# State space stage and branch projection of a streaming encoder layer, rewritten as one program in fixed order

## The chip, the cores and the metric

The kernel runs on one core of one Trainium2 chip. The metric is the device time of one execution in microseconds (us). Several runs of a kernel are taken and the median is given; one execution more is recorded by the hardware profiler, with the start of every instruction.

The engines are written as in the profile: PE (TensorE, matrix products; PEld its weight loads), DVE (VectorE), ACT (ScalarE), POOL (GpSimd), SP (SyncE, which here only issues DMAs). Each engine works through its own queue in order and waits for others by semaphores.

## What is computed

One layer of a hybrid trunk, for 256 frames of a new stream and 8 x 16 frames of running streams: 384 tokens in all, model width 2048, fp32.

```
u = rmsnorm(x)
proj = u @ w_in                      # pool | z | xBC | dt | gates
A = pooling branch(pool part)
xBC = silu(causal_conv(xBC) + b)     # width 4, per channel
x, B, C = split(xBC)                 # 64 heads of 64, 8 groups, state 128
y, h = ssd_scan(x, dt, A, B, C, h0)  # h: one 64x128 state a head
y = y + d_skip * x
y = rmsnorm over each group of 512 (y * silu(z)) * gain
m = sigmoid(gA) * (A @ w_pool_proj) + sigmoid(gB) * (y @ w_ssd_proj)
x += rmsnorm(m @ w_out)
x += rmsnorm(relu(rmsnorm(x) @ w_up)**2 @ w_down)
```

The scan of a group and chunk: `cb = C Bt`; for each head `Y = (cb * decay) @ (x dt) + exp(cum) * (C @ h)`; `h = h * exp(last) + Bt @ (x dt w_end)`. Outputs are the two token blocks and the new pooling, convolution and scan states.

## The kernel before

**Layout.** Activations lie transposed: a tile is 128 channels x 384 tokens, 256 of the new stream and 8 x 16 of the running ones. Every large product is done in two fp32r parts for accuracy: weights and activations are each split into a high part (ACT copy to fp32r) and a low part (DVE difference), and three products high x high, high x low, low x high are accumulated (`mm3`, L79 to L82). A *unit* is 512 KB of weights, 128x1024: SP fetches it (`wfetch`, L61), ACT and DVE split it (`wsplit`, L66 to L73), TensorE does 8 x 3 products of 384 columns with it (`half`, L84). Three buffers serve each of raw, high and low weights.

**Stages.** Pooling branch and gate A; then the state space stage (`phd`, from L371); then the branch projection (`phe`, from L612: 16 tiles of 4 units each, merged with the gates); then `w_out`; then the MLP. The state space stage goes through 8 groups. In each: conv tiles B and C, four conv tiles x (`conv`, L390: scale by rstd, four taps, Silu), four z tiles, one gate B tile in the first six groups (`NG = 6`), two units each. The last ten gate tiles come at the end.

**Short products.** When a group's tiles are there, plain fp32 products follow: the transposes of B (`trB`, L437), `cb` = B x C (L461), and for each of four pairs of heads j the transposes of x (`trx`, L480), `yi` = C x state (L514, in four strips of 32 columns), `Y` (L531, two strips of 64 columns; the scaled `yis` is added by a product with the identity, L539), and `pp`, the new prompt state (L560). An fp32 product appears in the trace as two records. After every second pair, `xhl` goes through DRAM (`x_scr`) into the strided tile `xst`, and eight fp32r products `su` (L587) update 1 MB of running states `hs`, which is stored and its buffer loaded anew. `b_scr` and `bst` do the same for B. The decays E are made per head by one ACT Exp, three DVE differences (L499), and two Exps for the pair; DVE multiplies them by the masked `cb` (L509).

**Norm of a group.** `finish` (L592) calls `rms_bc` (L113): three fp32 products of the sum of squares with two columns of ones (`st`, L116), Newton's steps for 1/sqrt on a 128x3 tile, three diagonal tiles `dg`, one fp32 product of ones with them (`bc`, L125) that spreads the result over the partitions; then four DVE products scale z into `a_scr` in DRAM.

**Order.** In all of this the order of instructions on each engine is not the program's: a scheduler places them by its own estimates of when operands are ready and of priority, so short products fall between units of dense ones wherever it finds them ready. Only the MLP runs in written order, under `tc.manual_schedule()`. PSUM's eight banks are four for long products (`mm`) and four for short ones (`ss`).

Of the kernel before, what the change touches and what calls it, by code (L numbers as in the profile page):

```python
# [27 lines left out]
NG = 6  # L28
# [6 lines left out]
def build(ctx, tc, io):  # L35
# [5 lines left out]
    psm = ctx.enter_context(tc.tile_pool(name="psm", bufs=4, space=PSUM))  # L41
    pss = ctx.enter_context(tc.tile_pool(name="pss", bufs=4, space=PSUM))
# [7 lines left out]
    def mmtile(name):  # L50
        return psm.tile([P, 512], F32, tag="mm", name=name)

    def sstile(name):
        return pss.tile([P, 512], F32, tag="ss", name=name)
# [20 lines left out]

    def wload(src, name):
        return wsplit(wfetch(src, name))
# [293 lines left out]
    with tc.tile_pool(name="phd", bufs=2, reuse_waits="tile") as pd, tc.tile_pool(  # L371
        name="phd1", bufs=1, reuse_waits="tile"
    ) as pd1:
        bst = []
        for i in range(2):
            b = pd1.tile([P, 4, 2, P], F32R, name=f"bst{i}")
            gp.memset(b.bitcast(F32), 0.0)
            bst.append(b)
        cst_ = pd1.tile([P, 48, 9, 3], F32, name="cstate")
        gp.dma_start(cst_, io["state_conv"])  # L380
        cbuf = []
        for i in range(3):
            b = pd1.tile([P, 24, 19], F32, name=f"cbuf{i}")
            gp.memset(b[:, 0, :3], 0.0)
            cbuf.append(b)
        seg = lambda a: a.rearrange("p (b t) -> p b t", b=24)
        ncv = [0]

        def conv(ui, c, tag, nb):
            ps = proj(in_units(ui), xg, f"x{c}")  # L390
            b = cbuf[ncv[0] % 3]
            ncv[0] += 1
            v.tensor_tensor(b[:, :, 3:], seg(ps), seg(rstd), ALU.mult)
            s.copy(b[:, 16:, :3], cst_[:, c, 1:])
            s.copy(b[:, 1:16, :3], b[:, 0:15, 16:])
            s.copy(cst_[:, c], b[:, 15:, 16:])
            a = pd.tile([P, T], F32, tag="cacc", name=f"cacc{c}")
            w = lambda j: vec[:, V_CW + c * 4 + j : V_CW + c * 4 + j + 1]
            v.tensor_scalar(seg(a), b[:, :, 0:16], w(0), None, ALU.mult)
            for j in range(1, 4):  # L400
                v.scalar_tensor_tensor(
                    out=seg(a), in0=b[:, :, j : j + 16], scalar=w(j), in1=seg(a), op0=ALU.mult, op1=ALU.add
                )
            o = pd.tile([P, T], F32, tag=tag, name=f"xs{c}", bufs=nb)
            s.activation(o, a, AF.Silu, bias=vec[:, V_CB + c : V_CB + c + 1])
            return o

        gates = list(range(16))

        def gate_b():  # L410
            n = gates.pop(0)
            ps = proj(in_units(33 + n), xg, f"gb{n}")
# [5 lines left out]
        for g in range(G):  # L418
            u0 = 49 + g * 10
            BT = conv(u0, 32 + g, "BT", 2)  # L420
            CT = conv(u0 + 1, 40 + g, "CT", 2)
            xs = []
            for j in range(4):
                xs.append(conv(u0 + 2 + j, g * 4 + j, "xs", 6))
                if g and j == 2:
                    finish(last[0])
            zs = []
            for j in range(4):
                ps = proj(in_units(u0 + 6 + j), xg, f"z{g}_{j}")
                z = pd.tile([P, T], F32, tag="zs", name=f"zs{g}_{j}", bufs=7)  # L430
                v.tensor_tensor(z, ps, rstd, ALU.mult)
                s.activation(z, z, AF.Silu)
                zs.append(z)

            tr = sstile(f"trB{g}")
            for b in range(3):
                te.transpose(tr[:, b * P : b * P + P], BT[:, b * P : b * P + P], ident)  # L437
            Bk = pd.tile([P, 2, P], F32, tag="Bk", name=f"Bk{g}")
            s.copy(Bk.rearrange("p b n -> p (b n)"), tr[:, :TP])
            Bhl = pd.tile([P, 2, P], F32R, tag="Bhl", name=f"Bhl{g}", bufs=1)  # L440
            s.activation(Bhl[:, 0, :], tr[:, TP:T], AF.Copy)
            v.tensor_tensor(Bhl[:, 1, :], tr[:, TP:T], Bhl[:, 0, :].bitcast(F32), ALU.subtract)
            bscr = b_scr[g]
            sy.dma_start(bscr, Bhl.bitcast(F32))
            bs = bst[g % 2]
            for p4 in range(4):
                for h2 in range(2):
                    sy.dma_start(
                        bs[p4 * 32 + h2 * 16 : p4 * 32 + h2 * 16 + 16, :, h2, :].bitcast(F32),
                        bscr.rearrange("(q h r) l n -> h l r q n", q=4, h=2)[h2, p4 // 2],  # L450
                    )
            Cm = pd.tile([P, 2, P], F32, tag="Cm", name=f"Cm{g}")
            v.tensor_tensor(
# [14 lines left out]
            for j in range(4):  # L468
# [10 lines left out]
                for b in range(3):  # L479
                    te.transpose(tr[:, b * P : b * P + P], xs[j][:, b * P : b * P + P], ident)  # L480
# [124 lines left out]
        while gates:  # L605
            gate_b()
# [612 lines left out]
```

## Time and profile before

| | |
|---|---|
| runs | 2835.02, 2835.99, 2837.01 us |
| median | 2835.99 us |
| profiled execution | 2835.97 us, of which span 2834.2 us |
| PE busy | 2811.6 us, 99% of the span |
| DVE busy | 1797.7 us, 63% |
| ACT busy | 1278.2 us, 45% |
| POOL busy | 251.2 us, 9% |
| mean DMA rate | 174 GB/s |

The span is the time from the first to the last instruction of the profiled execution; what lies around it belongs to the launch. A row of instructions reads: line, engine, operation, tile written <- tiles read (buffer numbers left out), shape, count | busy us, mean ns of one | idle time of the engine before them and what ended it. Matmul records overlap, since they are pipelined: their starts are measured, their ends are modelled. So the price of a product is the time from its start to the next one's start, not its length. A row of stages gives the stretch, its length, and each engine's busy time with the number of instructions in the order PE, PEld, DVE, ACT, POOL, then TensorE's granted clock, the DMA share and GB/s.

### The profile page before, as it was taken

The page shows a single profiled execution, that of the slowest core. Times are in us where ns is not written, and L with a number is a line of the kernel's source. Part 1 is how long each engine was busy: PE and PEld are TensorE (multiplying, and loading weights), DVE is VectorE, ACT ScalarE, POOL GpSimd, SP SyncE. Part 2 cuts the span into 40 slices and gives each one's busy share as a digit, 9 for nine tenths or more (in the row PEclk, how much of TensorE's full clock was granted, in tenths as well). Part 3 has the DMA queues.
Part 4 walks back from the last instruction along what each step waited for, and adds up shares of the span by engine and source line. Part 5 has one row for each costly group of instructions (what it writes and reads, how often), then busy time and mean ns, then how long its engine had stood idle before and what let it go on. Part 6 is the DMA issues. An engine that isn't in the chain of part 4 may idle for free.

```text
span 2834.2 us, 40535 instructions
## 1 busy us (share of the span) xinstructions
PE 2811.6 (99%) x15997; PEld 2655.8 (94%) x15997; DVE 1797.7 (63%) x2504; ACT 1278.2 (45%) x1866; POOL 251.2 (9%) x321
## 2 busy tenths in 40 slices
PE   9999999999999999999999999999999999999998
PEld 8999999999999999999999988899999999999996
DVE  7774335678677677686633333666767677676766
ACT  5443224345445455343522223545555555555553
POOL 0000000011011011011000000000111111111111
PEclk9999999999999999999999999999999999999999
DMA  6444445466465465565744454445666656666656
GB/s 212 134 133 142 138 138 196 142 208 208 148 219 193 158 224 178 169 234 185 244 149 149 154 182 130 149 167 172 186 184 158 163 160 167 167 180 188 182 131 233
DMA packets 160784, 492.90 MB, mean 174 GB/s; under 512 B 19809, under 2 KB 43553, under 8 KB 155729
## 3 DMA queue, kind: packets, MB, share of 16 engines
q1 hardware_dynamic: 133296, 410.14, 43.8%
q0 software_dynamic: 27296, 80.18, 11.8%
q8 instruction: 125, 2.05, 0.3%
q14 instruction: 67, 0.54, 0.1%
HBM read 412.34 MB, written 77.89 MB: 173 GB/s over the span
## 4 chain that ended last, share of the span: by engine, by line
PE 97%; DVE 1%; DMA 0%; ACT 0%; issue 0%; SPq 0%; DVEq 0%; ACTq 0%
PE pj_up L80 6%; PE pj_up L81 6%; PE pj_up L82 6%; PE pj_x L82 5%; PE pj_x L80 5%; PE pj_x L81 5%; PE wd L914 3%; PE pj_sp L80 3%; PE wd L916 3%; PE pj_z L82 3%; PE wd L915 3%; PE pj_z L80 3%; PE pj_sp L81 3%; PE pj_z L81 3%; PE pj_sp L82 3%; PE t L914 2%
## 5 line engine op out<-in xcount | busy, mean ns | idle before, releaser
L80 PE MATMUL pj_up<-x1h,wh_up 128*128 128x384 f32 x1024 | 345.6, 338 | 0.0
L81 PE MATMUL pj_up<-x1l,wh_up 128*128 128x384 f32 x1024 | 345.2, 337 | 0.0
L82 PE MATMUL pj_up<-x1h,wl_up 128*128 128x384 f32 x1024 | 344.6, 337 | 0.0
L80 PE MATMUL pj_x<-xgh,wh_x 128*128 128x384 f32 x768 | 261.4, 340 | 0.0
L82 PE MATMUL pj_x<-xgh,wl_x 128*128 128x384 f32 x768 | 258.3, 336 | 0.0
L81 PE MATMUL pj_x<-xgl,wh_x 128*128 128x384 f32 x768 | 256.9, 334 | 0.0
L73 DVE TENSOR_TENSOR wl_wd<-raw,wh_wd 128x1024 fp32r<-128x1024 f32 x168 | 202.2, 1222 | 68.9 <-ACT wh_wd L71 65.3
L71 ACT ACTIVATE wh_wd<-raw 128x1024 fp32r<-128x1024 f32 x168 | 175.1, 1054 | 97.0 <-PE pj_up L81 84.3
L80 PEld LDWEIGHTS pj_up<-x1h,wh_up 128*128 128x128 f32 x1024 | 192.8, 188 | 4.8 <-ACT x1h L732 0.4
L81 PEld LDWEIGHTS pj_up<-x1l,wh_up 128*128 128x128 f32 x1024 | 192.8, 188 | 4.5
L82 PEld LDWEIGHTS pj_up<-x1h,wl_up 128*128 128x128 f32 x1024 | 192.7, 188 | 0.1
L82 PE MATMUL pj_z<-xgh,wl_z 128*128 128x384 f32 x512 | 171.0, 334 | 0.0
L80 PE MATMUL pj_z<-xgh,wh_z 128*128 128x384 f32 x512 | 171.0, 334 | 0.0
L82 PE MATMUL pj_sp<-abh,wl_sp 128*128 128x384 f32 x512 | 171.0, 334 | 0.0
L81 PE MATMUL pj_z<-xgl,wh_z 128*128 128x384 f32 x512 | 171.0, 334 | 0.0
L80 PE MATMUL pj_sp<-abh,wh_sp 128*128 128x384 f32 x512 | 171.0, 334 | 0.0
L81 PE MATMUL pj_sp<-abl,wh_sp 128*128 128x384 f32 x512 | 171.0, 334 | 0.0
L73 DVE TENSOR_TENSOR wl_sp<-w_sp,wh_sp 128x1024 fp32r<-128x1024 f32 x64 | 78.2, 1224 | 118.3 <-ACT wh_sp L71 117.9
L882 POOL DMA_DIRECT2D acc_scr<-ev x108 | 92.9, 930 | 667.7 <-ACT ev L878 650.8
L80 PEld LDWEIGHTS pj_x<-xgh,wh_x 128*128 128x128 f32 x768 | 144.3, 188 | 2.5 <-issue 1.4
L82 PEld LDWEIGHTS pj_x<-xgh,wl_x 128*128 128x128 f32 x768 | 144.2, 188 | 2.6 <-issue 2.6
L81 PEld LDWEIGHTS pj_x<-xgl,wh_x 128*128 128x128 f32 x768 | 144.3, 188 | 1.1 <-issue 0.2
(344 smaller groups left out, 7106.8 us busy)
## 6 DMA issues: line engine op xcount, KB each, us to landing
w_up<-w_up SPq DMA_DIRECT2D x128, 512.0 KB, 4.5
raw<-w_down SPq DMA_DIRECT2D x112, 512.0 KB, 7.2
w_x<-w_in SPq DMA_DIRECT2D x96, 512.0 KB, 3.7
w_z<-w_in SPq DMA_DIRECT2D x64, 512.0 KB, 3.5
w_sp<-w_ssd SPq DMA_DIRECT2D x64, 512.0 KB, 3.5
acc_scr<-ev POOLq DMA_DIRECT2D x126, 256.0 KB, 4.5
w_ga<-w_in SPq DMA_DIRECT2D x32, 512.0 KB, 3.4
w_pp<-w_pp SPq DMA_DIRECT2D x32, 512.0 KB, 3.4
```

The costliest lines, as they stand in the source:

```text
L71: s.activation(h, w, AF.Copy)
L73: v.tensor_tensor(l, w, h.bitcast(F32), ALU.subtract)
L80: te.matmul(out, wh, xh, start=first, stop=False)
L81: te.matmul(out, wh, xl, start=False, stop=False)
L82: return te.matmul(out, wl, xh, start=False, stop=last)
L882: gp.dma_start(acc_scr[p][r], e, accum_op=ALU.add)
L914: te.matmul(o, ah, wh[:, c], start=first, stop=False)
L915: te.matmul(o, ah, wl[:, c], start=False, stop=False)
L916: te.matmul(o, al, wh[:, c], start=False, stop=fin)
```

## The change

The state space stage and the branch projection become one list of items, worked off in written order under `tc.manual_schedule()`:

- `flow` runs the list. An item is a unit (fetch, split, products, what follows) or a call. Fetches are issued 4 units ahead, splits 3 ahead (2 after `narrow`); every fourth split has buffers of its own (`wturn`). After each unit `work` takes work for DVE and ACT from a queue `todo`, by listed costs, up to 2.6 us; `need` takes out what a next item requires.
- The short products of a group go into two blocks, `block(old, new)`. Each does `Y` for the pairs of heads prepared by the block before (`old`), and the transposes and `yi` for the next two pairs (`new`); a group's first block also `trB` and `cb`. The order on TensorE is written out: Y, Y, yi, yi, yis by the identity, pp, trx, then trB and cb.
- A group's norm is two fp32r products of ones (128x128) with the high and low part of the sum of squares, 384 columns, one accumulation; Newton's steps run on the whole 128x384 tile (`norm_mm`).
- The differences for E become ACT Relu with scale -1 and bias, and Exp with scale -1. The first conv tap moves from DVE to ACT. The sum of squares moves from POOL to DVE.
- One `bst` instead of two; `hs`, `cbc`, `xst` and `bst` are loaded by items at given places. `NG` is 7, and the last block, update and norm stand between the last nine gate tiles.
- PSUM is 2 `mm` and 6 `ss` banks in this part, and 4 and 4 again after it. The branch projection's operands are loaded 7 ahead and split from `todo`; the first two units of `w_out` are fetched and split within the list (`ready`).

The core of the diff:

```diff
-NG = 6
+NG = 7
...
+    def work(budget):
+        debt[0] += budget
+        while todo and debt[0] > 0:
+            cost, _, f = todo.popleft()
+            f()
+            debt[0] -= cost
+        debt[0] = min(debt[0], 0.0)
+
+    def need(*tags):
+        while any(t in tags for _, t, _ in todo):
+            cost, _, f = todo.popleft()
+            f()
+            debt[0] -= cost
+
...
+        def prep(i):
+            i += 3 if wide[0] is not None else 2
+            while done[0] < min(i, n):
+                hl[done[0]] = units[done[0]][1](got[done[0]])
+                done[0] += 1
+
+        def begin():
+            for i in range(far):
+                fetch(i)
+            prep(0)
+
+        def rest():
+            i = -1
+            for x in items:
+                if not isinstance(x, tuple):
+                    x()
+                    continue
+                i += 1
+                if x[2] is None:
+                    continue
+                fetch(i + far)
+                x[2](hl[i])
+                prep(i + 1)
+                x[3]()
+                work(budget)
+                hl[i] = got[i] = None
+
+        return begin, rest
 
...
+    def block(old, new):
+        Y = []
+        if old:
+            g, hf = old
+            need(f"E{g}_{hf * 2}", f"E{g}_{hf * 2 + 1}")
+            d = S[g]
+            for j in (hf * 2, hf * 2 + 1):
+                y = sstile(f"Y{g}_{j}")
+                Y.append(y)
+                for sb, e0, c0, n in ((0, 0, 0, TP), (1, TP, P, P), (2, T, TP, P)):
+                    for hh in range(2):
+                        te.matmul(
+                            y[hh * 64 : hh * 64 + 64, c0 : c0 + n],
+                            d["xdt"][j][:, sb, hh * 64 : hh * 64 + 64],
+                            d["E"][j][:, hh, e0 : e0 + n],
+                            start=sb == 0,
+                            stop=False,
+                            skip_group_check=True,
                         )
+        if new:
+            g2, h2 = new
+            d2 = S[g2]
+            j0 = h2 * 2
+            if h2 == 0:
+                need(f"x{32 + g2}", f"x{40 + g2}")
+            need(f"x{g2 * 4 + j0}", f"x{g2 * 4 + j0 + 1}")
+            hs = d2["hs"][h2]
+            yi = sstile(f"yi{g2}_{h2}")
+            for j2 in range(2):
                 for c in range(4):
                     for r in range(2):
                         te.matmul(
+                            yi[c * 32 : c * 32 + 32, j2 * P : j2 * P + P],
+                            d2["Cm"][:, r, c * 32 : c * 32 + 32],
                             hs[:, 2 * c + r, j2 * P : j2 * P + P],
                             start=r == 0,
                             stop=r == 1,
                         )
+        if old:
+            for y, j2 in zip(Y, range(2)):
+                te.matmul(y[:, TP:T], d["yis"][hf][:, j2 * P : j2 * P + P], ident, start=False, stop=True, skip_group_check=True)
+            pp = sstile(f"pp{g}_{hf}")
+            for j2 in range(2):
                 for b in range(2):
+                    te.matmul(pp[:, j2 * P : j2 * P + P], d["xdw"][hf][:, j2, b, :], d["Bk"][:, b, :], start=b == 0, stop=b == 1)
+        trx = []
+        if new:
+            for j in (j0, j0 + 1):
+                tr = sstile(f"trx{g2}_{j}")
+                trx.append(tr)
+                for b in range(3):
+                    te.transpose(tr[:, b * P : b * P + P], d2["xs"][j][:, b * P : b * P + P], ident)
+            if h2 == 0:
+                BT, CT = d2["BT"], d2["CT"]
+                trB = sstile(f"trB{g2}")
+                for b in range(3):
+                    te.transpose(trB[:, b * P : b * P + P], BT[:, b * P : b * P + P], ident)
+                cb = sstile(f"cb{g2}")
+                for sb, t0, c0, n in ((0, 0, 0, 256), (1, P, 256, P), (2, TP, T, P)):
+                    te.matmul(cb[:, c0 : c0 + n], BT[:, sb * P : sb * P + P], CT[:, t0 : t0 + n], start=True, stop=True)
+        if new:
+            yis = d2["yis"][h2] = pd.tile([P, 2 * P], F32, tag="yis", name=f"yis{g2}_{h2}")
+            hd = g2 * 8 + h2 * 4
+            v.tensor_tensor(
+                yis.rearrange("p (h q) -> p h q", h=4),
+                yi[:, : 2 * P].rearrange("p (h q) -> p h q", h=4),
+                tok[:, 10, hd : hd + 4].unsqueeze(2).to_broadcast([P, 4, 64]),
+                ALU.mult,
+            )
+        if old:
+            for y, j in zip(Y, (hf * 2, hf * 2 + 1)):
+                x = d["xs"][j]
+                i = V_DSK + g * 4 + j
+                v.scalar_tensor_tensor(out=x, in0=x, scalar=vec[:, i : i + 1], in1=y[:, :T], op0=ALU.mult, op1=ALU.add)
+            pe = pd.tile([P, 2 * P], F32, tag="pe", name=f"pe{g}_{hf}", bufs=1)
+            s.copy(pe, pp[:, : 2 * P])
+            for j2 in range(2):
+                gp.dma_start(io["new_ssm_p"][g * 4 + hf * 2 + j2], pe[:, j2 * P : j2 * P + P])
+        if new:
+            xdw = d2["xdw"][h2] = pd.tile([P, 2, 3, P], F32, tag="xdw", name=f"xdw{g2}_{h2}", bufs=1)
+            for j2, tr in enumerate(trx):
+                xdt = d2["xdt"][j0 + j2] = pd.tile([P, 3, P], F32, tag="xdt", name=f"xdt{g2}_{j0 + j2}")
+                tv = tr[:, :T].rearrange("p (b h q) -> p b h q", b=3, h=2)
+                for o, i in ((xdt, 3), (xdw[:, j2], 6)):
                     v.tensor_tensor(
+                        o.rearrange("p b (h q) -> p b h q", h=2),
+                        tv,
+                        tok[:, i : i + 3, hd + j2 * 2 : hd + j2 * 2 + 2].unsqueeze(3).to_broadcast([P, 3, 2, 64]),
                         ALU.mult,
                     )
+            if h2 == 0:
+                Bk = d2["Bk"] = pd.tile([P, 2, P], F32, tag="Bk", name=f"Bk{g2}", bufs=1)
+                s.copy(Bk.rearrange("p b n -> p (b n)"), trB[:, :TP])
+                Bhl = pd.tile([P, 2, P], F32R, tag="Bhl", name=f"Bhl{g2}", bufs=1)
+                s.activation(Bhl[:, 0, :], trB[:, TP:T], AF.Copy)
+                v.tensor_tensor(Bhl[:, 1, :], trB[:, TP:T], Bhl[:, 0, :].bitcast(F32), ALU.subtract)
+                sy.dma_start(b_scr[g2], Bhl.bitcast(F32))
+                cbm = d2["cbm"] = pd.tile([P, 512], F32, tag="cbm", name=f"cbm{g2}", bufs=1)
+                v.tensor_tensor(cbm, cb, cst2[:, :512], ALU.mult)
+        if new:
+            state_tasks(g2, h2)
+            decay_tasks(g2, h2)
+            decay_state(g2, h2)
+        if old:
+            gated_tasks(g, hf)
+        if new:
+            decay_masks(g2, h2)
+
...
+            def head(hh, j=j, h0=h0):
+                if hh == 0:
+                    d["E"][j] = pd.tile([P, 2, 512], F32, tag="E", name=f"E{g}_{j}")
+                E, cbc, h = d["E"][j], d["cbc"][j], h0 + hh
+                s.activation(E[:, hh, P:TP], cbc[:, hh, P:TP], AF.Exp, bias=tok[:, 9, h : h + 1])
+                for b, e0 in enumerate((0, TP, T)):
+                    s.activation(
+                        E[:, hh, e0 : e0 + P], cbc[:, hh, b * P : b * P + P], AF.Relu, bias=tok[:, b, h : h + 1], scale=-1.0
                     )
+
+            def powers(j=j):
+                E = d["E"][j]
+                s.activation(E[:, :, :P], E[:, :, :P], AF.Exp, scale=-1.0)
+                s.activation(E[:, :, TP:], E[:, :, TP:], AF.Exp, scale=-1.0)
+
...
+    def norm_mm(g):
+        need(f"sum{g}")
+        d = S[g]
+        bc = sstile(f"bc_g{g}")[:, :T]
+        te.matmul(bc, onesr, d["sh"], start=True, stop=False)
+        te.matmul(bc, onesr, d["sl"], start=False, stop=True)
+        ms = pd.tile([P, T], F32, tag="ms", name=f"ms_g{g}", bufs=1)
+        y = pd.tile([P, T], F32, tag="ssum", name=f"nwy_g{g}", bufs=1)
+        a = pd.tile([P, T], F32, tag="ysq", name=f"nwa_g{g}", bufs=1)
+
...
+    def bst_load(g):
+        for p4 in range(4):
+            for h2 in range(2):
+                sy.dma_start(
+                    bst[p4 * 32 + h2 * 16 : p4 * 32 + h2 * 16 + 16, :, h2, :].bitcast(F32),
+                    b_scr[g].rearrange("(q h r) l n -> h l r q n", q=4, h=2)[h2, p4 // 2],
+                )
+
+    def xst_load(g, hf):
+        need(f"xhl{g}_{hf}")
+        xst = S[g]["xst"] = pd.tile([P, 4, 2 * P], F32R, tag="xst", name=f"xst{g}_{hf}", bufs=1)
+        for p4 in range(4):
+            sy.dma_start(
+                xst[p4 * 32 : p4 * 32 + 32].bitcast(F32),
+                x_scr[g * 2 + hf].rearrange("(q r) l j n -> l r q (j n)", q=4)[p4 % 2],
+            )
+
...
+    for g in range(G):
+        u0 = 49 + g * 10
+        xu = lambda j: conv_units(u0 + 2 + j, g * 4 + j, "xs", 6, put(g, "xs", j))
+        items += conv_units(u0, 32 + g, "BT", 1, put(g, "BT"))
+        if g:
+            at(xst_load, g - 1, 1)
+        items += conv_units(u0 + 1, 40 + g, "CT", 1, put(g, "CT"), lambda g=g: make_Cm(g))
+        u = xu(0)
+        items += u[:1]
+        if g:
+            at(update, g - 1, 1)
+        items += u[1:]
+        at(cbc_load, g, 0)
+        items += xu(1) + xu(2)
+        at(block, (g - 1, 1) if g else None, (g, 0))
+        u = xu(3)
+        items += u[:1]
+        at(lambda g=g: (need(f"su{g - 1}_1"), hs_load(g, 1)))
+        items += u[1:]
+        at(bst_load, g)
+        at(xst_load, g, 0)
+        items += z_units(g, 0)
+        u = z_units(g, 1)
+        items += u[:1]
+        at(update, g, 0)
+        items += u[1:]
+        if g:
+            at(norm_mm, g - 1)
+        items += z_units(g, 2)
+        u = z_units(g, 3)
+        items += u[:1]
+        at(cbc_load, g, 1)
+        items += u[1:]
+        at(block, (g, 0), (g, 1))
+        if g < G - 1:
+            at(lambda g=g: (need(f"su{g}_0"), hs_load(g + 1, 0)))
             if g < NG:
+                items += gate_units(gates.pop(0))
+
...
+    tail_ = [x for u in last_gates for x in u]
+    items += tail_[:2]
+    at(xst_load, G - 1, 1)
+    items += tail_[2:4]
+    at(block, (G - 1, 1), None)
+    at(narrow)
+    items += tail_[4:5]
+    at(update, G - 1, 1)
+    items += tail_[5:8]
+    at(norm_mm, G - 1)
+    items += tail_[8:11]
+    at(branch_open)
+    items += tail_[11:]
+
...
+    begin, rest = flow(items)
+    begin()
+    with tc.manual_schedule():
+        banks(mm=2, ss=6)
+        rest()
```

More of the change, by code (lines that the diff above doesn't have):

```diff
@@ L369, in build @@
             gp.dma_start(ma_scr[n], m)
[L371 to L391, printed above, removed]
+    nothing = lambda *_: None
@@ L400, in conv @@
[L400 to L412, printed above, removed]
+            s.activation(seg(a), b[:, :, 0:16], AF.Copy, scale=w(0))
```

461 lines of the change are left out of this document (269 added, 192 removed).

## Prediction

> **What bounds the kernel now.** I read the page's summary first, then a table by stage, then the tile views of the long products, then TensorE's timeline.
>
> ```profile
> span 2834.2 us, 40535 instructions
> ```
>
> ```profile
> PE 2811.6 (99%) x15997; PEld 2655.8 (94%) x15997; DVE 1797.7 (63%) x2504; ACT 1278.2 (45%) x1866; POOL 251.2 (9%) x321
> ```
>
> ```profile
> 456.00:1390.00 934.00, 933.66 (x6059) 897.03 (x6058) 673.49 (x1175) 443.61 (x756) 109.25 (x127) 1.00 0.59 195
> 1390.00:1657.00 267.00, 267.00 (x1542) 266.91 (x1541) 107.09 (x121) 81.02 (x90) 0.54 (x1) 1.00 0.49 154
> ```
>
> TensorE (first two busy columns: PE, PEld; then DVE, ACT, POOL) works without a gap in both stages that are rewritten, at granted clock 1.00. So no wait can be removed there: time comes only from what the matmuls cost. A busy PE is not a cheap PE, however; the price of each kind follows from start times.
>
> ```profile
> L80 PE MATMUL pj_x<-xgh,wh_x x768: 334/334/637, 456.4 to 1256.2; 128*128 128x384 f32 x192
> ```
>
> ```profile
> L80 PE MATMUL pj_sp<-abh,wh_sp x512: 334/334/334, 1390.3 to 1656.0; 128*128 128x384 f32 x171
> ```
>
> In the branch projection 512 triples start between 1390.3 and 1656.0: 265.7 / 511 / 3 = 0.1733 us per 128x384 product. I call that the dense pace (24 products, one unit of weights, take 4.16 us); the branch projection already runs at it, so I give its rewrite no gain. The state space stage lasts from 456.4 to 1390.3, 933.9 us, and holds 48 + 32 + 16 output tiles (conv, z, gate) of 48 products: 4608 x 0.1733 = 798.7. The other **135.2 us are what the short products add**, and they are what the change can touch.
>
> **What the short products cost.** Columns below: start, length, operation. A step is the difference of two starts; what a run adds is its steps, with those of its dense neighbours, less the dense pace.
>
> ```profile
> 604.59 0.33 PE L82 MATMUL pj_x<-xgh,wl_x 128*128 128x384 f32 x1
> 604.76 0.73 PE L116 MATMUL st_g<-cst,ssum 128*128 128x2 f32 x6
> 605.35 0.42 PE L80 MATMUL pj_x<-xgh,wh_x 128*128 128x384 f32 x1
> 605.61 0.34 PE L81 MATMUL pj_x<-xgl,wh_x 128*128 128x384 f32 x1
> ```
>
> ```profile
> 612.54 0.34 PE L82 MATMUL pj_x<-xgh,wl_x 128*128 128x384 f32 x1
> 612.93 0.88 PE L125 MATMUL bc_g<-dg_g,cst 128*128 128x384 f32 x2
> 613.35 0.63 PE L80 MATMUL pj_x<-xgh,wh_x 128*128 128x384 f32 x1
> 613.82 0.33 PE L81 MATMUL pj_x<-xgl,wh_x 128*128 128x384 f32 x1
> ```
>
> ```profile
> 563.54 0.33 PE L80 MATMUL pj_x<-xgh,wh_x 128*128 128x384 f32 x1
> 563.72 1.11 PE L587 MATMUL su<-xst,bst 128*128 128x256 f32 x8
> 564.66 0.34 PE L81 MATMUL pj_x<-xgl,wh_x 128*128 128x384 f32 x1
> 564.84 0.34 PE L82 MATMUL pj_x<-xgh,wl_x 128*128 128x384 f32 x1
> ```
>
> The norm's two places: 605.61 - 604.59 - 0.35 = 0.67 and 613.82 - 612.54 - 0.35 = 0.93, so 1.60 a group, 12.8 in all. A state update: 1.30 - 0.35 = 0.95, 16 of them 15.2. That leaves 135.2 - 12.8 - 15.2 = 107.2 us, 13.4 a group, for the scan's products.
>
> ```profile
> 539.63 0.49 PE L437 MATMUL trB<-cst,xs 128*128 128x128 f32 x3
> 539.96 1.04 PE L461 MATMUL cb<-xs,xs 128*128 128x256 f32 x6
> 540.84 0.49 PE L480 MATMUL trx<-cst,xs 128*128 128x128 f32 x3
> ```
>
> ```profile
> 545.08 0.34 PE L80 MATMUL pj_gb<-xgh,wh_gb 128*128 128x384 f32 x1
> 545.35 1.09 PE L531 MATMUL Y<-E,xdt 128*64 128x256 f32 x12
> 546.37 0.49 PE L539 MATMUL Y<-cst,yis 128*128 128x128 f32 x2
> 546.70 0.61 PE L560 MATMUL pp<-Bk,xdw 128*128 128x128 f32 x4
> 547.14 0.49 PE L480 MATMUL trx<-cst,xs 128*128 128x128 f32 x3
> 547.56 0.66 PE L514 MATMUL yi<-hs,Cm 128*32 128x128 f32 x16
> 548.16 0.44 PE L81 MATMUL pj_gb<-xgl,wh_gb 128*128 128x384 f32 x1
> 548.44 0.34 PE L82 MATMUL pj_gb<-xgh,wl_gb 128*128 128x384 f32 x1
> ```
>
> Between full-array products nothing is lost: trB takes 0.33 for three, cb 0.88, pp 0.44 for four, 0.11 a record. Each passage between full array and column strips (Y's 128*64, yi's 128*32) costs: dense to Y 0.27, 0.10 over pace; trx 0.42 when yi follows, 0.09 over; the first dense product after yi 0.28, 0.11 over. A record of this size is 0.27 long (trB: 0.49 less two steps of 0.11), so the last Y starts 0.82 after the first and its exit takes 0.20, twice an inner step; the last yi starts 0.39 after its first and exits in 0.21; the two yis records take 0.33 where two of pp take 0.22. Today each of 32 head pairs passes in and out of the strips for Y and again for yi.
>
> **The change, part by part.** *Blocks.* The count of short products stays; two calls of `block` a group put them in one order: Y, Y, yi, yi, then the four yis records, pp, six trx, and in the group's first block trB and cb. The sum for one: entry 0.10; two Y at 0.92 (1.02 less the 0.10 of an exit not paid) 1.84; Y to yi 0.05; yi 0.39 + 0.07 + 0.39 + 0.21 = 1.06; yis 0.22 + 3 x 0.11 = 0.55; pp 8 x 0.11 = 0.89; trx 0.66. That is 5.15, and 6.36 with trB and cb: 11.51 a group, 92.1, plus 0.3 because the first and last block are halves. **Saved: 107.2 - 92.4 = 14.8 us.** The passage Y to yi is in no row: its lower bound is nothing in place of the inner step I counted (-0.10), its upper a passage like the others (+0.11); I take 0.05, about 1.6 us either way over 16 blocks. The Trainium skill (TensorEngine Tiling (Array Packing), Key Properties) says that changing the tiling mode drains TensorE, and 64- and 32-column strips are two modes: by that, this term sits near its upper end and the time is about 1 us later. The rows on passages bear the rule out; none here shows this one.
>
> *Norms.* Six st and two bc records become two fp32r products of 384 columns, the very form of the dense ones: 2 x 0.1733 and 0.01 for the return (as after su), 0.36 a group. **Saved 8 x (1.60 - 0.36) = 9.9 us.** Upper bound: a return like bc's (613.35 to 613.82 is 0.30 over pace) would take 0.5 x 8 = 4 back; lower bound nothing beyond pace. I take the low end, since su, also fp32r, returns without loss. The state updates keep form and number: 0.
>
> *DVE and ACT.* Their work changes hands.
>
> ```profile
> L499 DVE TENSOR_SCALAR E<-cbc,tok 128x128 f32<-128x128 f32 x192 | 50.9, 316 | 1.2 <-DMA cbc<-cum_scr 1.2
> ```
>
> ```profile
> L495 ACT ACTIVATE E<-cbc,tok 128x128 f32<-128x128 f32 x64 | 24.7, 398 | 5.7 <-ACT xhl L491 2.7 <-PE Y L531 2.2 <-DMA cbc<-cum_scr 0.7
> L495 ACT ACT_TABLE_LOAD x17 | 21.8, 1283 | 13.7 <-DVE E L509 6.9 <-PE Y L531 6.7
> L508 ACT ACTIVATE E<-E 128x512 f32<-128x512 f32 x32 | 20.1, 628 | 2.1 <-DVE E L499 2.1
> ```
>
> ```profile
> L542 DVE SCALAR_TENSOR_TENSOR xs<-xs,vec,Y 128x384 f32<-128x384 f32 x32 | 19.5, 609 | 7.6 <-PE Y L539 7.6
> ```
>
> DVE gives up 192 differences (50.9) and 48 first taps; it takes the squares' sums from POOL (24) and Newton's steps on whole 128x384 tiles, 11 a group: at no more than 0.61 each, (24 + 88) x 0.61 = 68. It stays near 690 of some 910, and weight splits run three units (12.5 us) ahead of TensorE, so I cost it at 0. ACT takes the 192 as Relu, at the bound of the Exp of that shape 192 x 0.398 = 76, and 48 taps at most 0.63, 30: 444 + 106 = 550, 60%. Again 0, under the same lead; without it every late split would stall TensorE in full. The Trainium skill (ScalarE: Activation LUTs, Rules for kernel authors) wants relu and min on VectorE instead; the rows agree that the piece is slower on ACT (398 against 316 ns), and by the rule the 25 us more would count only if ACT were the bound.
>
> *New waits.* Six `ss` banks serve eight tiles in a first block: trB waits until DVE has read the first Y (L542, 0.61), cb the second. Queued behind are TensorE's remaining products and all dense ones. The yis records start 3.05 into the block, trB is due at 5.15 and cb at 5.48. DVE first finishes the conv tile before the block: eviction 0.61, about 0.8 for ACT's part, three taps 1.83; then it reads yi and both Y, 0.61 each: the first Y is free at 4.5, the second at 5.1. I take 0.2 x 7 = 1.4; a DVE two us late makes it 14. Turning to and from the fixed order (PSUM pools changed twice): 1.0.
>
> **Sum:** 2835.97 for the profiled execution (span 2834.2; median of the runs 2835.99) - 14.8 - 9.9 + 1.4 + 1.0 = **2813.7 us**.
>
> **Rivals.** (1) *Passages are not saved*: drains come back inside blocks, or waits for yis or banks eat them. Then only the norms are left, 2835.97 - 9.9 + 2.4 = 2828.5. For it: no row shows such a block; against: pp, trx, cb follow each other at 0.11.
>
> (2) *SP holds the weights, and the kernel is slower.*
>
> ```profile
> SPq L474 <- DMA new_ssm_s<-hs: 71.5, 14, 10.3
> ```
>
> ```profile
> L571 SPq DMA_DIRECT2D xst<-x_scr x64: 303/423/1278, 554.1 to 1329.6; - x64
> ```
>
> ```profile
> w_x<-w_in SPq DMA_DIRECT2D x96, 512.0 KB, 3.7
> ```
>
> ```profile
> L73 DVE TENSOR_TENSOR wl_x<-w_x,wh_x 128x1024 fp32r<-128x1024 f32 x96 | 115.9, 1217 | 23.4 <-ACT wh_x L71 23.3
> ```
>
> The second half's state load now stands in program order between weight fetches, followed by eight bst and four xst gathers. If it waits its longest 10.3 for the store of the half before, and the gathers take 12 x 0.42, a fetch is 15.3 late. Fetched four units ahead (16.6 us), it needs 3.7 to land and about 2.4 for both splits: 10.5 spare. TensorE stalls 4.8 in each of 8 groups: 2813.7 + 38 = 2852. It decides from a hold of 10.5 us. Against it: the store is six units old by then.
>
> (3) *Relu needs a table of its own.* Then a pair's Exp and Relu pieces need nine loads instead of one, 8 x 1.28 = 10.3 more before the next weight split. That queue (16 pieces at 0.40, four at most 0.63, one load) leaves about 3 us of lead by my count; 7 x 16 = 115 more gives 2929. Against it: Copy and Square between the Exps show no load. The Trainium skill (the same page, Table sets: the hidden batching unit) has relu as filler in every set, which would rule this out; no trace here has a Relu to show it.
>
> **How the numbers follow.** Forecast 0.66 (2807 to 2821: the Y to yi bound, 4 for the norm's return, a few us of bank waits); rival 1 0.17; rival 2 0.10, a third of it so mild that the time is unchanged; rival 3 0.04; unnamed stalls beyond these 0.03. Faster by over 0.2% (5.7 us, what a measurement can tell): 0.66 + 0.15 of rival 1 + 0.01 = 0.82; within it 0.02 of rival 1 and 0.03 of rival 2; slower 0.07 + 0.04 + 0.02 = 0.13. The range, 2807 to 2834, leaves out some 0.05 below and 0.15 above.
>
> **What would show it.** The stage should run from 456 to about 910 us later, with the branch projection still 266 long; per group two stretches of about 5 and 6 us without dense products; bc of two records, next dense start 0.35 later; no st. Steps inside a block show Y to yi directly. Wrong would be: idle time of PE before Y, trB or su (rivals 1, 2), before L80 to L82 with wl or DMA as releaser (rival 2), or table loads at the Relu lines (rival 3).

## The result, and the profile after

| | before | after |
|---|---|---|
| median of four runs | 2835.63 us | 2812.88 us |
| lowest and highest | 2835.02, 2837.01 | 2811.83, 2813.74 |
| profiled span | 2834.2 us | 2811.4 us |

After to before is 0.9919, 95% interval 0.9902 to 0.9936: 22.75 us less, where the forecast was 22.3 less. The summary of the changed kernel's page:

```profile
span 2811.4 us, 40219 instructions
...
PE 2787.5 (99%) x15949; PEld 2658.0 (95%) x15949; DVE 1768.2 (63%) x2233; ACT 1323.7 (47%) x2063; POOL 196.1 (7%) x295
```

TensorE is still busy 99% of the time; it is busy 24.1 us less. The tile view (min/median/max ns of one, first and last start) gives the borders of the stages, as it did for the kernel before:

```profile
L168 PE MATMUL pj_x<-xgh,wh_x x768: 333/334/419, 455.4 to 1244.3; 128*128 128x384 f32 x192
...
L168 PE MATMUL pj_sp<-abh,wh_sp x512: 333/334/335, 1371.1 to 1636.8; 128*128 128x384 f32 x171
...
L993 PE MATMUL wo<-wh_wo,mh x192: 387/389/390, 1637.3 to 1767.2; 128*128 128x512 f32 x192
```

`pj_x` opens the state space stage, `pj_sp` the branch projection, `wo` the `w_out` stage, whose end is the first product of the MLP at 1767.9. From the same rows of the kernel before (456.4, 1390.3, 1656.5, 1790.9) follows a bill by stage:

| | before | after | difference |
|---|---|---|---|
| start of the state space stage | 456.4 | 455.4 | -1.0 |
| state space stage | 933.9 | 915.7 | -18.2 |
| branch projection | 266.2 | 266.2 | 0.0 |
| `w_out` | 134.4 | 130.6 | -3.8 |
| the rest, to the end of the span | 1043.3 | 1043.5 | +0.2 |

The stage that was rewritten gave 18.2. The other 3.8 came in a stage whose instructions hardly changed; that was not foreseen. The start differs by 1.0, ahead of the change; its size is that of the spread between runs (two other versions of the kernel before, in experiments 1 and 8, start the stage at 455.0 and 455.8).

**A block.** TensorE's timeline around a second block of a group, then the end of a first one (start, length, operation):

```profile
542.45 0.34 PE L170 MATMUL pj_z<-xgh,wl_z 128*128 128x384 f32 x1
542.72 1.96 PE L568 MATMUL Y<-E,xdt 128*64 128x256 f32 x24
544.61 1.12 PE L588 MATMUL yi<-hs,Cm 128*32 128x128 f32 x32
545.65 0.71 PE L597 MATMUL Y<-cst,yis 128*128 128x128 f32 x4
546.20 1.06 PE L601 MATMUL pp<-Bk,xdw 128*128 128x128 f32 x8
547.10 0.82 PE L608 MATMUL trx<-cst,xs 128*128 128x128 f32 x6
547.67 0.42 PE L168 MATMUL pj_gb<-xgh,wh_gb 128*128 128x384 f32 x1
547.93 0.34 PE L169 MATMUL pj_gb<-xgl,wh_gb 128*128 128x384 f32 x1
...
603.76 0.49 PE L613 MATMUL trB<-cst,xs 128*128 128x128 f32 x3
604.09 1.04 PE L616 MATMUL cb<-xs,xs 128*128 128x256 f32 x6
604.88 0.42 PE L168 MATMUL pj_x<-xgh,wh_x 128*128 128x384 f32 x1
```

No row carries an idle time, and the block enters the strips once and leaves them once. 547.93 - 542.45 - 2 x 0.1733 = 5.13 us is what it adds over the dense pace. The same sum for every run of short products in the trace:

```
count  adds, us   what
  8     5.133     second block of a group
  7     6.346     first block (with trB and cb)
  1     3.073     the very first, a half block
  1    10.276     the very last, a half block
  8     0.353     norm: two bc products
 16     0.953     state update su
```

One line stands out: **the last half block costs 10.28 us** where its products make 3.43. (3.43 is that block's own price without a wait; experiments 3 and 6 below measure it.)

**The norm** is now two products among dense ones, with the next dense start 0.36 after the first bc:

```profile
630.89 0.34 PE L757 MATMUL bc_g<-sh,onesr 128*128 128x384 f32 x1
631.07 0.34 PE L758 MATMUL bc_g<-sl,onesr 128*128 128x384 f32 x1
631.25 0.33 PE L168 MATMUL pj_z<-xgh,wh_z 128*128 128x384 f32 x1
```

**The one wait.** In the view of waits TensorE has a single row from the start of the state space stage to the end of the branch projection (us in total, times, longest):

```profile
PE Y L568 <- DVE E L749: 3.8, 2, 2.1
```

Both waits are in the last block, for the two masked decay tiles E. The rows around it from the timelines of TensorE, ACT and DVE (in brackets: idle time before, and what ended it):

```profile
1301.04 0.34 PE L170 MATMUL pj_gb<-xgh,wl_gb 128*128 128x384 f32 x1
1303.08 1.09 PE L568 MATMUL Y<-E,xdt 128*64 128x256 f32 x12 [1.70 <-DVE E L749]
1306.30 1.97 PE L568 MATMUL Y<-E,xdt 128*64 128x256 f32 x12 [2.14 <-DVE E L749]
...
1287.10 1.28 ACT L729 ACT_TABLE_LOAD   x1
...
1294.23 0.62 ACT L738 ACTIVATE E<-E 128x512 f32<-128x512 f32 x1
1294.75 1.05 ACT L82 ACTIVATE wh_gb<-w_gb 128x1024 fp32r<-128x1024 f32 x1
...
1295.83 1.23 DVE L84 TENSOR_TENSOR wl_gb<-w_gb,wh_gb 128x1024 fp32r<-128x1024 f32 x1 [7.73 <-ACT wh_gb L82]
...
1301.71 1.22 DVE L749 TENSOR_TENSOR E<-E,cbm 128x1024 f32<-128x1024 f32 x1
...
1304.94 1.21 DVE L749 TENSOR_TENSOR E<-E,cbm 128x1024 f32<-128x1024 f32 x1
```

Read from the bottom: the masks ran at 1301.71 and 1304.94, behind weight splits and other work on DVE; DVE had stood idle for 7.73 us until ACT delivered a high part; ACT delivered it late because the table load and all the last pieces of E (1287.10 to 1294.75) stood ahead of it. ACT's row order, then, is the first suspect. Elsewhere two blocks lie some 50 us apart (542.45, 598.46, 647.71, ...); the last one starts 21.8 us after its forerunner (1279.27 to 1301.04), which would hide the same lateness there. TensorE's windows over these 16 us (stretch, length, PE, PEld, DVE, ACT and POOL busy, granted clock, DMA share, GB/s) show a second loss:

```profile
1301.00:1305.00 4.00, 1.47 (x15) 0.85 (x13) 3.60 (x6) 1.94 (x3) 0.00 (x0) 1.00 0.40 131
1305.00:1309.00 4.00, 2.70 (x15) 2.07 (x16) 1.16 (x2) 0.52 (x1) 0.54 (x1) 0.54 0.50 184
1309.00:1313.00 4.00, 4.00 (x20) 4.00 (x19) 3.08 (x6) 0.80 (x2) 1.06 (x2) 0.61 0.02 8
...
1305.40:1312.00 6.60, 5.70 (x28) 5.07 (x29) 2.83 (x6) 0.98 (x3) 0.70 (x2) 0.50 0.30 112
```

The granted clock falls to 0.54 and 0.61; the last row shows that it is 0.50 from 1305.4 to 1312.0, and that the rows of 4 us mix this with full clock. In that stretch pp steps by 0.213 us instead of 0.111. Of 10.28 - 3.43 = 6.85 us, the waits are 3.84 and the slow clock the remaining 3.0.

**`w_out`.** From the `wo` row: (1767.2 - 1637.3) / 191 / 3 = 0.2267 us a product. Before, from the same row of that kernel:

```profile
L652 PE MATMUL wo<-wh_wo,mh x192: 393/396/398, 1656.5 to 1790.2; 128*128 128x512 f32 x192
```

(1790.2 - 1656.5) / 191 / 3 = 0.2333. The 6.6 ns over 576 products are the 3.8 us. Count, form and order of the products are the same, at granted clock 1.00 in both. A line of the diff that the section on the change leaves out allocates a tile that nothing uses, after the last operand of `w_out`:

```diff
+            if n == KD - 1:
+                held["mpool"].tile([P, 120], F32, name="pad_mp")
```

The changed kernel has a second new tile that nothing uses, `pad_phd` of 64 columns in the state space stage. No run leaves it out, so what it is worth is not known.

### The profile page after: what moved, and what is told of

Read it like the earlier page. It is cut to its first block, busy times and chain, and to the rows that moved or that the text cites. A ratio compares the mean times of both kernels' runs of the same rounds, so it can differ in the third digit from the quotient of the medians.

```text
span 2811.4 us, 40219 instructions
## 1 busy us (share of the span) xinstructions
PE 2787.5 (99%) x15949; PEld 2658.0 (95%) x15949; DVE 1768.2 (63%) x2233; ACT 1323.7 (47%) x2063; POOL 196.1 (7%) x295
## 4 chain that ended last, share of the span: by engine, by line
PE 93%; DVE 3%; ACT 1%; issue 1%; DMA 0%; SPq 0%; DVEq 0%; ACTq 0%
PE pj_up L168 6%; PE pj_up L170 6%; PE pj_up L169 6%; PE pj_x L170 4%; PE pj_x L169 4%; PE pj_x L168 4%; PE wd L1255 3%; PE pj_sp L168 3%; PE wd L1257 3%; PE wd L1256 3%; PE pj_sp L169 3%; PE pj_sp L170 3%; PE pj_z L169 3%; PE pj_z L170 3%; PE pj_z L168 3%; PE t L1255 2%
```

## The experiments

Eight kernels, timed in two groups; the kernel before had median 2836.08 us on the chip of the first group (experiments 1, 3, 5 and 7) and 2835.58 on that of the second. Intervals are of the ratio to it.

**1. The norms alone**, in the kernel before, under its scheduler. To make room, `cbuf` has two buffers instead of three.

```diff
-                bc = rms_bc(pd, ssum, 512, f"g{g}", after)
+                s.activation(sh, ssum, AF.Copy)
+                v.tensor_tensor(sl, ssum, sh.bitcast(F32), ALU.subtract)
+                with behind(after):
+                    te.matmul(ob, onesr, sh, start=True, stop=False)
+                    te.matmul(ob, onesr, sl, start=False, stop=True)
```

> The kernel before with the norms alone changed (two fp32r products of ones, Newton on the whole tile; cbuf twice instead of three times for room). Theory: the norm's 1.60 us a group on TensorE falls to 0.36, 9.9 us in all, and DVE's added Newton steps are hidden: 2835.6 to 2825.7. Rival (the scheduler's order gives it back, by later splits or by short products that fall elsewhere): 2832 to 2836.

Measured 2826.13 us, ratio 0.9963 (0.9951 to 0.9976). The stage shrinks from 933.9 to 923.7, so 10.1, and the bc runs add 0.384 on average; the branch projection takes 0.8 more (267.0). The norm's term stands by itself.

**2. The passages.** In the changed kernel, `yi` goes from behind Y to the end of the block: one more passage out of the strips and one more in, same products.

```diff
-            yi = sstile(f"yi{g2}_{h2}")
...
         if old:
...
+            yi = sstile(f"yi{g2}_{h2}")
...
+            yis = d2["yis"][h2] = pd.tile([P, 2 * P], F32, tag="yis", name=f"yis{g2}_{h2}")
```

> The changed kernel with the strips' products of a block parted: Y, Y, yis, pp, trx (trB, cb), and yi, yi last, next to the dense products; DVE reads yi after both Y. Nothing is left out and each block is still one stretch. Theory (passages): a block saves because it enters and leaves the column strips once for two pairs; parted, Y and yi each go in and out, so a block rises by about 0.2 us, 5.13 to 5.33 and 6.35 to 6.55, and the time by about 3 us, to 2816. Rival (what saves is that no dense product stands between the short ones): 5.13 and 6.35 stay, 2812.9.

Measured 2829.64 us, ratio 0.9981 (0.9972 to 0.999). The second blocks, where nothing waits, cost 5.333 instead of 5.133: 0.20 for the extra passages, as the passage theory has it. The total missed, since this order brought waits that the theory did not have. TensorE's rows in the view of waits for the stage:

```profile
PE Y L568 <- DVE E L750: 3.9, 2, 2.0
PE cb L604 <- DVE xs L622: 3.3, 7, 0.5
PE bc_g L758 <- ACT sh L712: 2.7, 7, 0.7
PE bc_g L759 <- DVE sl L713: 0.5, 3, 0.2
```

The first row is the last block's, as before. In each of seven first blocks `cb` waits 0.5 for a bank until DVE has read Y; with this and the extra passages a first block costs 7.27 (6.346 + 0.92). The norm's operand is late too, 1.30 instead of 0.353. 8 x 0.2 + 7 x 0.92 + 8 x 0.95 = 15.6 of the stage's 15.3 more (931.0). So the bank wait that the prediction priced at 0.2 a block is real in this order; in the changed kernel's own order it does not bind.

**3. Where the last wait comes from: distance.** The tail's calls stand two units later.

```diff
-    items += tail_[2:4]
+    items += tail_[2:6]
     at(block, (G - 1, 1), None)
     at(narrow)
-    items += tail_[4:5]
+    items += tail_[6:7]
     at(update, G - 1, 1)
-    items += tail_[5:8]
+    items += tail_[7:10]
     at(norm_mm, G - 1)
-    items += tail_[8:11]
+    items += tail_[10:13]
     at(branch_open)
-    items += tail_[11:]
+    items += tail_[13:]
```

> The changed kernel with its last block (group 7, second half, no new pairs), update, norm and branch opening each two units later among the last gate tiles. Theory (distance): that block waits for its masked decays only because four units, 16.6 us, lie between it and the block before, where the others have ten or more; two units later both waits (1.70 and 2.14 us) and the clock drop behind them are gone: about 8.4 us less, 2812.9 to 2804.5, the block itself at about 2 us in place of 10.3. Rival (DVE and ACT are behind by then in any case, so that the wait moves along): 2811 to 2814.

Measured 2812.46 us, ratio 0.9914 (0.9901 to 0.9928): no gain beyond the changed kernel. The time is in the rival's range, but not for the rival's reason: the block's waits are gone, it costs 3.430 and the stage 909.8, 5.9 less. The branch projection gives back 4.6 (270.8). Rows of the view of waits around its start:

```profile
ACT abh L890 <- DMA ar<-a_scr: 8.1, 4, 4.1
DVE abl L891 <- ACT abh L890: 7.0, 5, 3.3
...
PE pj_sp L169 <- DVE abl L891: 1.0, 2, 0.9
...
PE pj_sp L168 <- ACT abh L890: 0.7, 1, 0.7
```

and the windows at that place:

```profile
1375.00:1380.00 5.00, 4.33 (x25) 4.00 (x24) 1.78 (x4) 0.88 (x3) 0.00 (x0) 1.00 0.99 349
1380.00:1385.00 5.00, 3.77 (x13) 2.95 (x14) 4.46 (x8) 4.07 (x7) 0.00 (x0) 0.84 0.95 343
```

`branch_open` begins to load the branch projection's operands. The DMA engines are full here (share 0.95 to 0.99), but they are so in the changed kernel too (0.96 from 1375 to 1380), where nothing waits. What differs is the distance: the last of the 32 loads is issued 12.1 us after the projection's first product, in the changed kernel 3.8 us after it. The new waits are on the operand parts, and the clock follows: from 1383.35 to 1386.8 products start every 0.32 us instead of 0.173, which is some 1.6 of the 4.6 us; the waits and the late starts around them are the other 3.0. Distance cures the last block; the rest of the tail cannot be shifted with it for nothing.

**4. Only the block, the update and the norm later**, `branch_open` where it was (block after 6 tail units, update 7, norm 9, open 11).

```diff
-    items += tail_[2:4]
+    items += tail_[2:6]
...
-    items += tail_[5:8]
+    items += tail_[7:9]
...
-    items += tail_[8:11]
+    items += tail_[9:11]
```

> The changed kernel with the last block and update two units later and its norm one unit later, but the branch opening left where it was. When all four were moved, the block's wait went (stage 915.7 to 909.8) and the branch projection grew by 4.6 (266.2 to 270.8). Theory (the late opening crowded 32 operand loads and their splits into the projection's first units): with the opening in place the projection is 266 to 267 and the time 2806 to 2808. Rival (the norm behind the later block is what comes late): 2810 to 2813.

Measured 2810.11 us, ratio 0.9908 (0.9894 to 0.9921): the theory's 2806 to 2808 missed, and the lower edge of the rival's range. The stage is 909.7, the branch projection 267.9 with one wait left:

```profile
PE pj_sp L169 <- DVE abl L891: 0.9, 1, 0.9
```

Opening in place takes back 2.9 of the 4.6. The remaining 1.7 goes with the norm, which now stands 37.6 us before the projection's first product instead of 41.8: the first operand load is issued as early as before, but the last one 9.6 us after that product, between the 3.8 of the changed kernel and the 12.1 of experiment 3. This speaks for the rival; it was not tried by itself.

**5. Where the last wait comes from: ACT's burst.** The differences go back to DVE as they were before; ACT does only the Exps.

```diff
-                    s.activation(
-                        E[:, hh, e0 : e0 + P], cbc[:, hh, b * P : b * P + P], AF.Relu, bias=tok[:, b, h : h + 1], scale=-1.0
+                    v.tensor_scalar(
+                        E[:, hh, e0 : e0 + P],
+                        cbc[:, hh, b * P : b * P + P],
+                        tok[:, b, h : h + 1],
+                        0.0,
+                        ALU.subtract,
+                        ALU.min,
...
-                s.activation(E[:, :, :P], E[:, :, :P], AF.Exp, scale=-1.0)
-                s.activation(E[:, :, TP:], E[:, :, TP:], AF.Exp, scale=-1.0)
+                s.activation(E[:, :, :P], E[:, :, :P], AF.Exp)
+                s.activation(E[:, :, TP:], E[:, :, TP:], AF.Exp)
```

> The changed kernel with the decays' differences back on DVE (subtract and min, Exp without the scale) in place of Relu on ACT. Theory (ACT's burst): in the last block the masks are late because 16 decay pieces, 8 us on ACT, stand ahead of a weight split for which DVE waits 7.7 us; with the burst at some 4 us the masks come 4 us earlier and most of the 8.4 us go: 2804 to 2809, the other blocks unchanged at 5.13 and 6.35. Rival (DVE is what is late): DVE gets 51 us more, the wait stays or grows: 2813 to 2818.

Measured 2807.44 us, ratio 0.9897 (0.9883 to 0.991). This is in the theory's range. The other blocks keep their 5.133 and 6.346; the last one costs 4.513. ACT's and TensorE's rows at that place:

```profile
1287.30 1.28 ACT L729 ACT_TABLE_LOAD   x1
...
1291.46 1.04 ACT L82 ACTIVATE wh_gb<-w_gb 128x1024 fp32r<-128x1024 f32 x1
...
1303.69 1.09 PE L568 MATMUL Y<-E,xdt 128*64 128x256 f32 x12 [0.85 <-DVE E L754]
```

From the table load to the weight split it is 4.2 us instead of 7.65, the split starts 3.3 earlier, one of the two waits is gone, the other is 0.85, and the granted clock stays at 1.00. The stage takes 910.1, 5.6 less than in the changed kernel.

**6. Both: differences on DVE, and the block one unit later** (block 5, update 6, norm 8, open 11).

> The changed kernel with the differences on DVE (as tried before, 2807.4) and the last block and update one unit later; norm and branch opening stay where they are. Theory (ACT's burst and distance together): what is left of the last block's wait, 0.9 us, goes, its 4.5 becomes 3.4 as where nothing waits, and the branch projection stays at 266.3, since its operands are loaded as early as before: 2805.5 to 2806.5. Rival (the norm then stands too close behind the block): the wait moves to bc or to the branch projection, 2807 to 2812.

Measured 2807.11 us, ratio 0.9898 (0.9885 to 0.9912). The median is 0.6 above the theory's range and at the lower edge of the rival's; the profiled execution, 2805.93, is inside the theory's, and its trace shows no wait of the rival's kind. Windows of the two stages:

```profile
456.00:1364.00 908.00, 908.00 (x6005) 892.80 (x6004) 681.95 (x1095) 435.65 (x759) 54.53 (x101) 1.00 0.59 198
1364.00:1630.00 266.00, 266.00 (x1537) 266.00 (x1536) 109.99 (x121) 79.28 (x90) 0.54 (x1) 1.00 0.48 160
```

TensorE has no wait at all here. The last block costs 3.431, the stage (first `pj_x` 455.4, first `pj_sp` 1364.2) 908.8. That is the sum of its products: 798.7 dense + 16 x 0.953 + 8 x 5.133 + 7 x 6.346 + 8 x 0.353 + 3.073 + 3.431 = 908.8. The one unit of distance is worth 1.3 us of the stage in the profiled executions (910.1 to 908.8) and cannot be told from experiment 5 in the medians; either of the two is the best version seen, 28 us under the kernel before.

**7 and 8. The unused tile**, taken from the changed kernel, and given to the kernel before:

```diff
-            if n == KD - 1:
-                held["mpool"].tile([P, 120], F32, name="pad_mp")
```

> The changed kernel without the unused tile of 120 columns behind the merged operands. The products of w_out start every 227 ns in the changed kernel and every 230 to 235 ns before, 3.8 us over 576 products. Theory (place in SBUF): the tile moves the operands; without it the pace is 230 to 235 again and the time 2816 to 2817. Rival (the pace comes from the fixed order, from weights at hand or from PSUM's banks): 227 stays and so do 2812.9.

```diff
             ms_.append((h, l))
+        mp.tile([P, 120], F32, name="pad_mp")
```

> The kernel before with the unused tile of 120 columns behind the merged operands of w_out, nothing else. Theory (place in SBUF): the products of w_out start every 227 ns in place of 230 to 235, the stage from 134.4 to 130.6 us, the time from 2836 to 2832. Rival (pad and fixed order are needed together): 2836.

Without it: 2817.16 us, ratio 0.993 (0.9917 to 0.9944). With it alone: 2831.67, ratio 0.9985 (0.9976 to 0.9994). The `wo` row of the changed kernel without the tile:

```profile
L991 PE MATMUL wo<-wh_wo,mh x192: 393/396/398, 1637.9 to 1771.6; 128*128 128x512 f32 x192
```

and of the kernel before with it:

```profile
L653 PE MATMUL wo<-wh_wo,mh x192: 387/389/390, 1655.8 to 1785.7; 128*128 128x512 f32 x192
```

1771.6 - 1637.9 = 133.7, and 1785.7 - 1655.8 = 129.9: each kernel takes the pace of the other. In both pairs TensorE, DVE, ACT and POOL work off the same instructions in the same order with the tile and without it. The gain in `w_out` is the tile's, in both directions, and has nothing to do with blocks or order.

## Why the prediction was right, and where not

**Blocks: right.** Priced at 5.15 and 6.36, measured 5.133 and 6.346; the seventeen blocks make 92.0 (with the last at 3.43, its price without waits) against the 92.4 of the sum, so 15.2 were saved instead of 14.8. That a whole block could be priced from the steps of the kernel before, which had no such block, is the main thing that held. The passage Y to yi, in no row of before, was taken as 0.05 with bounds of -0.10 and +0.11. The single starts show it: the last Y of a block is followed by yi after 203 ns, inner steps of Y being 102. So it costs 0.10, the upper end. It did not show in the sum, because the second Y's first passes step by 209 ns where the first Y's first step is 260. The Trainium skill (TensorEngine Tiling (Array Packing), Key Properties) says that a change of tiling mode drains TensorE; by that rule this passage is one like the others, and the trace agrees, with 203 against 102 ns.

**Norms: right.** 0.36 a group predicted, 0.353 measured; the low end, no loss on the return, was the right choice. 10.0 saved instead of 9.9, and experiment 1 shows them alone.

**DVE and ACT at nothing: right for sixteen blocks, wrong for the last.** DVE is busy for 637.8 us in 911 us of the stage and ACT for 487.9, both less than the 690 and 550 I worked with, as this row of the windows shows, and no weight split stalls TensorE:

```profile
456.00:1367.00 911.00, 907.17 (x5983) 891.38 (x5982) 637.84 (x898) 487.89 (x946) 54.50 (x101) 1.00 0.57 196
```

The step that failed is "again 0, under the same lead": the lead I checked was that of the weight splits, three units, and a share of busy time. The lead of E was not checked, and it is not the same everywhere: some 50 us between blocks, 21.8 before the last. There ACT's burst of Exp and Relu, put before a split, came out on TensorE. By experiment 5 the move of the differences to ACT costs 5.6 us of the stage, all of it in one block. The Trainium skill (ScalarE: Activation LUTs, Rules for kernel authors) wants relu and min on VectorE; the prediction let the rule go because ACT was not the bound. The measurement agrees with the rule, though through the order of a queue and not through a rate.

**New waits: mechanism right, size and place wrong.** 1.4 for bank waits of trB and cb: measured 0 in all seven first blocks, since DVE was in time, if barely: in the first block shown above it had read the second Y at 603.96, and cb started at 604.09. 1.0 for turning to and from the fixed order: the branch projection opens without a wait. In place of these 2.4 stand 7.0 in the stage (6.95: 915.7 less the 908.75 that its products make up): 3.84 of waits for E, 3.0 of slow clock, and 0.1 elsewhere. The prediction has no term for the clock. Experiment 2 shows that the bank wait was no phantom.

**Not in the prediction: the unused tile**, -3.8 us. The diff had its line; the prediction does not speak of it, which puts it at nothing.

The bill: -15.2 - 10.0 + 7.0 - 3.8 - 1.0 + 0.2 = -22.8, the difference of the two spans. The forecast's -14.8 - 9.9 + 2.4 is -22.3. The terms that carry it held; 4.6 more of waits and 3.8 from the tile, both unforeseen, nearly cancel, and the total looks better for it than the working was.

**The rivals.** (1) Passages not saved: refuted by the blocks' price. (2) SP holds the weights: refuted. In the view of waits the state load (L540) stands behind the store of the half before once, for 1.1 us and not 10.3, the gathers after it (L786) for 3.0 at the longest, and TensorE has no wait on weights:

```profile
SPq L653 <- DVE Bhl L652: 111.3, 8, 14.7
...
SPq L786 <- DMA hs<-ssm: 19.6, 8, 3.0
...
SPq L540 <- DMA new_ssm_s<-hs: 1.1, 1, 1.1
```

The first row, a hold of 14.7 that the prediction did not have, is longer than the 10.5 from which I had it decide, and still TensorE did not wait. The trace shows what was left: each fetch of the stage was issued at least 9.0 us before the first product with its unit's low part (18.9 in the median), and each split ended at least 2.1 us before it. So the holds do take lead, and that point was set too low. (3) Relu with a table of its own: refuted by the row of the Relu line, 192 pieces of 387 ns, while the Exp line before it has the loads, two a group (its price in the prediction has a slip, 7 x 16 is 112 and not 115; nothing hangs on it):

```profile
L731 ACT ACTIVATE E<-cbc,tok x192: 385/387/391, 504.9 to 1293.6; 128x128 f32<-128x128 f32 x192
```

```profile
L729 ACT ACT_TABLE_LOAD x16 | 20.5, 1283 | 0.3
```

## What to carry to other kernels

Price a block of mixed matmuls by steps between starts, with each passage between full array and strips as a term of its own; it held within 0.02 us. When an edit gives work to an engine with room, do not ask only whether the engine becomes the bound: look for the place where the distance between producer and user is shortest, here the end of the loop, and follow what the added pieces stand in front of there. And when a forecast comes out right, make up the bill by stage all the same: two errors of about 4 us stood here behind a total right within about 0.5.

## What was not expected of the hardware

- **The pace of a product changed with a tile that nothing uses.** An unused tile of 120 fp32 columns changes a 128x512 product of `w_out` from 0.2333 to 0.2267 us, in two kernels and in both directions, with the instructions of the engines and their order the same. What is left for it to change is addresses; that is argued and not shown. Which operand's address it is, and by what mechanism, was not tried and stays open.
- **Short waits were enough for a lower clock.** In the changed kernel waits of 1.70 and 2.14 us, with 1.1 us of products between them, went with half the clock from 1305.4 to 1312.0, so from within the second wait on. In experiment 2, with waits of 1.97 and 1.93, half the clock was there before the second wait began:

```profile
1319.31 1.30 PE L568 MATMUL Y<-E,xdt 128*64 128x256 f32 x12 [1.97 <-DVE E L750]
...
1320.10:1320.60 0.50, 0.50 (x6) 0.10 (x2) 0.50 (x1) 0.00 (x0) 0.00 (x0) 0.50 0.01 0
```

In experiment 3 three waits of at most 0.9 us were followed by half pace for some 3.4 us, while the single waits of 0.85 in experiment 5 and 0.9 in experiment 4 left the clock at 1.00. The Trainium skill (TensorE: Matmul & The Clock Gate, HAM oscillation) gives the rule of no idle gaps above about 3.4 us; here no single gap reached that, so the measurement decides. What the clock goes by instead, no run isolates. The price of the two waits was 6.85 us and not 3.84; in the changed kernel without the unused tile the same two (1.69 and 2.13) cost 5.7, since the clock was low for only 3.4 us.
